# First weights of a seven-product group read from a copy at another SBUF place; ones kept as one column

## The chip, the cores and the metric

The kernel runs on one core of a Trainium2 chip. The metric is the device time of one execution in microseconds (us). A core has TensorE (PE, matrix products), VectorE (DVE), ScalarE (ACT), GpSimd (POOL) and SyncE (SP, which issues most transfers). A product on PE has two operands in SBUF: a stationary block of 128x128 weights, which is loaded first (PEld in the profile, overlapping the product before), and moving columns, which stream past it. Results go to PSUM.

## The reference, cut to what matters

The reference is a decoder trunk of two layers on 512 tokens with 1024 features, in float32. Each layer is: half a SwiGLU FFN, a mixer (gated linear attention, GLA, in the first layer; stick-breaking attention, SB, in the second), and half a SwiGLU FFN again, each behind an RMSNorm and added to x.

```python
def rmsnorm(x, g):
    y = x * lax.rsqrt(jnp.mean(x * x, axis=-1, keepdims=True) + EPS)
    return y * g

def swiglu(h, w_gate, w_up, w_down):
    return (jax.nn.silu(h @ w_gate) * (h @ w_up)) @ w_down

for i in range(2):
    x = x + 0.5 * swiglu(rmsnorm(x, ffn1_norm[i]), ffn1_w_gate[i], ffn1_w_up[i], ffn1_w_down[i])
    h = rmsnorm(x, mix_norm[i])
    x = x + (gla_mixer(h, ...) if i % 2 == 0 else sb_mixer(h, ...))
    x = x + 0.5 * swiglu(rmsnorm(x, ffn2_norm[i]), ffn2_w_gate[i], ffn2_w_up[i], ffn2_w_down[i])
return rmsnorm(x, final_norm)
```

w_gate and w_up are 1024x2816, w_down is 2816x1024. There are four FFNs in all.

## The kernel before, in words

x stays in SBUF transposed: eight tiles `x0` to `x7` of 128 features x 512 tokens. Every large product is made from three products of split operands: a tile is cut into a rounded part h (float32r) and the rest l, and W·B becomes Wh·Bh + Wl·Bh + Wh·Bl (`mm3`, whose products all carry line 62).

**The feed.** Weights pass through a queue of entries (`feed.q`), in the order in which the products are issued. An `Entry` has units, views of a chunk loaded by SP into `raw` (or `rawd` for the down projection). Before it is used, `Entry.split` cuts each unit: ACT casts it to `wh` (line 116), DVE subtracts to `wl` (line 118). `wh` and `wl` have four buffers each. `Feed.start` splits the entry at hand and up to two more behind it, at most four large units together, and begins to load chunks up to six entries ahead.

**Places.** A `wh` or `wl` buffer has 64 columns (256 bytes) to spare, and `place` says where in it the block begins: 0 for most entries, NEAR = 16 columns (64 bytes) for the entries of the seven-product form, NEAR_MOVING = 48 columns (192 bytes) for `tok` entries, where the weights' chunk is the moving operand. The tiles are laid out one behind the other, and all the large ones have sizes that are multiples of 256 bytes, or come behind such. So in this kernel an operand's place can be told by its address divided by 256: the remainder of a block at place 0 is that of the x, xh/xl, th/tl, nh/nl and hh/hl tiles, and is called remainder 0 here. Weights at NEAR have remainder 64, a `tok` chunk as moving operand has 192.

**An FFN.** The 2816 inner features are 11 chunks of 256, for gate and for up. The first three gate chunks and the first two up chunks go through `feat`: eight k-tiles of three products, 512 columns each (`ps_f`). All others go through `seven`: the product of a 2x2 block matrix of weights (256 features x 1024) with the 2x2 blocked input (1024 x 512 tokens) is computed with seven block products in place of eight (Winograd's form). Each block product is four k-tiles of three products with 256 columns, at line 500: 84 products a group, in PSUM tiles `ps_w`, `ps_z` and `ps_q`. A group has two entries:

- `body_1`: a11·n (ps_w), then sums s2 (ps_z), s1 (ps_q), then a12 (ps_w). Units: the chunk's first 128 columns and `sums_12`.
- `body_2`: s3 (ps_z), s4 (ps_q), a22 (ps_w). Units: `sums_34` and the last 128 columns of the chunk's second half.

DVE makes the sums of weight blocks (lines 485 to 492) and the sums of input blocks, which are split to `th`/`tl`. Between the groups stand entries of the down projection (`down`, product `ps_d`, 512 columns, 24 products an entry). So in the middle of an FFN PE does 84 products of 256 columns, 24 (or 48) of 512 columns, 84 of 256, and so on. There are 68 groups in the four FFNs; 52 follow a `ps_d` product, 4 a `ps_f` product and 12 another group directly.

**Ones.** `ones` is a 128x128 tile of 1.0, set by DVE at the start. It is the weights of `stats_b` (`ps_R`, spreads the norm factor over all partitions) and of the GLA output norm (`ps_on`), and its first column is the moving operand of `stats_a` (`ps_st`). `gT` (128x50) holds the norms' gains, copied from PSUM at the start; its first eight columns are used again by the last norm at the very end.

The SB layer's values and the GLA layer's use `tok` (`ps_t`): the input tile is the weights (remainder 0), the weights' chunk at NEAR_MOVING is the moving operand, 256 columns, three products a k-tile, 24 products a PSUM tile. In the GLA layer, `ps_gk` (the gate's first projection) has 512 columns with weights `gs`, a tile that by the sizes of those ahead of it has remainder 64.

Of the kernel before, what the change touches and what calls it, by code (L numbers as in the profile page):

```python
# [10 lines left out]
F32 = mybir.dt.float32  # L11
F32R = mybir.dt.float32r
# [6 lines left out]
P = 128  # L19
T = 512  # L20
D = 1024
KD = D // P
# [6 lines left out]
NEAR, NEAR_MOVING = 16, 48  # L29
# [3 lines left out]
def decoder(ctx: ExitStack, tc: tile.TileContext, a: dict, out: bass.AP):  # L33
    nc = tc.nc


    cp = ctx.enter_context(tc.tile_pool(name="cp", bufs=1))
    xp = ctx.enter_context(tc.tile_pool(name="xp", bufs=1))
    np_ = ctx.enter_context(tc.tile_pool(name="np", bufs=8))
    wp = ctx.enter_context(tc.tile_pool(name="wp", bufs=4))  # L40
# [6 lines left out]
    def psum(name, tag=None):  # L47
        if tag is None:
            tag = order[turn_[0] % 8]
            turn_[0] += 1  # L50
        return pp.tile([P, T], F32, tag=tag, bufs=banks[tag], name=name)
# [1 line left out]

    ident = cp.tile([P, P], F32, name="ident")
    make_identity(nc, ident)
    ones = cp.tile([P, P], F32, name="ones")
    nc.vector.memset(ones, 1.0)

    xs = [xp.tile([P, T], F32, name=f"x{k}") for k in range(KD)]

# [12 lines left out]
    class Chunk:  # L73
        def __init__(self, src, n, m):
            self.src, self.n, self.m, self.t = src, n, m, None
            self.pool = None
            self.few = False
# [12 lines left out]
    class Entry:  # L90
# [1 line left out]

        def __init__(self, units, body, place=0):
            self.units, self.body, self.W, self.place = units, body, None, place

        def split(self):
            if self.W is None:
                self.W = []  # L100
                for ch, view, n, m in self.units:
                    r = view(ch.load())
                    few = n * m < 1024
                    if few:

                        h = st["few"].tile([P, n * m + NEAR], F32R, tag="vh", bufs=1, name="wh")[:, NEAR:]
                        l = st["few"].tile([P, n * m + 64 - NEAR], F32R, tag="vl", bufs=1, name="wl")[:, : n * m]
                    else:
                        h, l = (
                            wp.tile([P, n * m + 64], F32R, tag="w" + t, bufs=4, name="w" + t)[  # L110
                                :, self.place : self.place + n * m
                            ]
                            for t in "hl"
                        )
                    h, l = (t.rearrange("p (n m) -> p n m", m=m) for t in (h, l))
                    st["cut"] = nc.scalar.copy(h, r).ins  # L116
                    with tc.issue_after(st["gains"]):
                        nc.vector.tensor_tensor(out=l, in0=r, in1=h.bitcast(F32), op=ALU.subtract)  # L118
                    self.W.append((h, l))

    class Feed:
        def __init__(self):
# [38 lines left out]
    feed = Feed()  # L161
# [162 lines left out]
    st = {}  # L324
# [89 lines left out]
    class FFN:  # L414
# [60 lines left out]
        def seven(self, ch, group=None):  # L475

            H = T // 2  # L480
            s12, v = [None], {}

            def sums_12(t):
                s = s12[0] = self.tp.tile([P, KD, P], F32, tag="s", bufs=4, name="s12")
                nc.vector.tensor_tensor(out=s[:, 0:4], in0=t[:, 0:4, P:], in1=t[:, 4:8, P:], op=ALU.add)
                nc.vector.tensor_tensor(out=s[:, 4:8], in0=s[:, 0:4], in1=t[:, 0:4, 0:P], op=ALU.subtract)
                return s

            def sums_34(t):
                s = self.tp.tile([P, KD, P], F32, tag="s", bufs=4, name="s34")  # L490
                nc.vector.tensor_tensor(out=s[:, 0:4], in0=t[:, 0:4, 0:P], in1=t[:, 0:4, P:], op=ALU.subtract)
                nc.vector.tensor_tensor(out=s[:, 4:8], in0=t[:, 4:8, 0:P], in1=s12[0][:, 4:8], op=ALU.subtract)
                return s

            def prod(o, w, w0, b, first=True):
                for j in range(4):
                    bh, bl = b(j)
                    wh, wl = w[0][:, w0 + j], w[1][:, w0 + j]
                    for n, (l_, r_) in enumerate(((wh, bh), (wl, bh), (wh, bl))):
                        nc.tensor.matmul(  # L500
                            o, l_, r_, start=first and j + n == 0, stop=j == 3 and n == 2, skip_group_check=True
                        )

            def half(k0, c):
                return lambda j: (st["h"][k0 + j][:, c * H : c * H + H], st["l"][k0 + j][:, c * H : c * H + H])

            def part(name):
                return self.tp.tile([P, H], F32, tag="c", bufs=2, name=name)

            def add(o, x, y):  # L510
                nc.vector.tensor_tensor(out=o, in0=x, in1=y, op=ALU.add)

            def left(o, w):
                if group is None:
                    nc.scalar.activation(o[:, 0:H], w, AF.Silu)
                else:
                    nc.vector.tensor_tensor(out=o[:, 0:H], in0=w, in1=self.gates[0][:, 0:H], op=ALU.mult)

            def rest(o, c):
                if group is None:  # L520
                    st["silu"] = nc.scalar.activation(o[:, c:T], o[:, c:T], AF.Silu).ins
                    self.gates.append(o)
                    return
                nc.vector.tensor_tensor(out=o[:, c:T], in0=o[:, c:T], in1=self.gates.pop(0)[:, c:T], op=ALU.mult)
                self.close(o, group)

            def body_1(W):
                ax, s = W

                v["w"], v["z"], v["q"] = psum("ps_w"), psum("ps_z"), psum("ps_q")  # L530
                w, z, q = (v[n][:, 0:H] for n in "wzq")
                v["o"] = self.tp.tile([P, T], F32, tag="t", name="o0")
                prod(w, ax, 0, half(0, 0))
                v["u2"] = part("u2")
                nc.scalar.copy(v["u2"], w)
                yield
                prod(z, s, 4, lambda j: self.t_half(1, j))
                add(v["u2"], z, v["u2"])
                yield
                prod(q, s, 0, lambda j: self.t_half(0, j))  # L540
                v["c5"] = part("c5")
                nc.scalar.copy(v["c5"], q)
                yield
                prod(w, ax, 4, half(4, 0), first=False)
                left(v["o"], w)
                yield

            def body_2(W):
                s, a22 = W
                q, y = v["q"][:, 0:H], v["z"][:, H:T]  # L550
                o0, o1 = v["o"], self.tp.tile([P, T], F32, tag="t", name="o1")
                prod(y, s, 0, lambda j: self.t_half(2, j))
                u3 = o1[:, 0:H]
                add(u3, y, v["u2"])
                nc.vector.tensor_tensor(out=o1[:, H:T], in0=u3, in1=v["c5"], op=ALU.add)
                yield
                prod(q, s, 4, half(4, 1), first=False)
                add(o0[:, H:T], q, v["u2"])
                rest(o0, H)
                yield  # L560
                o = v["w"][:, H:T]
                prod(o, a22, 0, lambda j: self.t_half(3, j))
                add(o1[:, 0:H], o, u3)
                rest(o1, 0)
                yield

            feed.q.append(Entry([(ch, lambda t: t[:, :, 0:P], KD, P), (ch, sums_12, KD, P)], body_1, NEAR))
            feed.q.append(Entry([(ch, sums_34, KD, P), (ch, lambda t: t[:, 4:8, P:], 4, P)], body_2, NEAR))

        def t_half(self, i, j):  # L570
# [575 lines left out]
                feed.entries(self.end + 2 - feed.pos)  # L1146

    gT = cp.tile([P, 50], F32, name="gT")  # L1150
    phases = []

    def ffn(n, i, gi, nxt, **kw):
# [49 lines left out]
    with tc.tile_pool(name="ip", bufs=1) as ip:  # L1203
# [10 lines left out]
        lead = phases[0].lead  # L1214
# [6 lines left out]
                c.load()  # L1221
        ps = psum("ps_g")
        nc.tensor.transpose(ps[:, 0:P], gl, ident)
        st["gains"] = nc.vector.tensor_copy(gT, ps[:, 0:50]).ins
        st["nh"], st["nl"], pst = [], [], []
        for hf in range(2):
            for k in range(hf * 4, hf * 4 + 4):
                ps = psum("ps_x")
# [73 lines left out]
```

## Time and profile before

| | us |
|---|---|
| median of 3 runs | 1896.93 (1896.65 to 1897.21) |
| the profiled execution | 1896.61 |
| its span | 1894.7 |
| PE busy | 1874.6 (99%) |
| weight loads busy (PEld) | 1672.7 (88%) |
| DVE busy | 1459.6 (77%) |
| ACT busy | 943.5 (50%) |
| mean granted TensorE clock | 0.998 |

The profiled execution is one run; 1.9 us of it lie outside the span. A line of a group reads: line of the kernel, engine, operation, out<-in by tile names, sizes and count, then the busy time in us, the mean ns of one, and the idle time of the engine just ahead of them. A line in order of time begins with the start and the duration in us. A matmul's duration contains its way through the array and overlaps the next one's, so how fast PE moves is read from start to start.

### The profile page before, as it was taken

The numbers are of one execution on the slowest core, as the hardware profiler recorded it, in microseconds if no ns is written. First come the engines' busy times: TensorE is split into PE (matmuls) and PEld (weight loads), VectorE is DVE, ScalarE is ACT, GpSimd is POOL, SyncE is SP. The second block draws the span as 40 slices with busy tenths as digits, with TensorE's granted clock in tenths as the row PEclk, the third lists the DMA queues.
The fourth block names the chain that finished last, engine by engine and source line by source line (L and its number), as shares of the span: only waits on it lengthen the run. The fifth ranks groups of instructions, "written<-read, shape, count | busy, mean of one in ns | idle before, by whom it ended". The sixth has DMA issues, their size and how long they took to land.

```text
span 1894.7 us, 28826 instructions
## 1 busy us (share of the span) xinstructions
PE 1874.6 (99%) x11789; PEld 1672.7 (88%) x11789; DVE 1459.6 (77%) x2313; ACT 943.5 (50%) x1450; POOL 7.4 (0%) x17
## 2 busy tenths in 40 slices
PE   8999999999999999999999999999999999999998
PEld 6899999889887899999989999998888788999997
DVE  7978777775766987877888778776878779777775
ACT  6534434444554544444453444445888755444444
POOL 0000000100000000000000000000000000000000
PEclk9999999999999999999999999999999999999999
DMA  5423333312223233332233333233221223333321
GB/s 156 145 91 110 101 112 96 91 46 67 67 67 111 89 90 113 106 116 79 78 112 122 101 100 108 82 90 100 67 67 58 66 90 104 107 101 103 119 80 67
DMA packets 177512, 179.02 MB, mean 94 GB/s; under 512 B 4034, under 2 KB 167924, under 8 KB 177380
## 3 DMA queue, kind: packets, MB, share of 16 engines
q1 hardware_dynamic: 176768, 176.18, 29.8%
q8 instruction: 92, 1.51, 0.3%
q0 software_dynamic: 512, 0.99, 0.2%
q14 instruction: 40, 0.33, 0.1%
q10 hardware_dynamic: 100, 0.03, 0.0%
HBM read 175.11 MB, written 2.10 MB: 94 GB/s over the span
## 4 chain that ended last, share of the span: by engine, by line
PE 96%; DVE 2%; ACT 1%; DMA 1%; issue 0%; DVEq 0%; ACTq 0%; SPq 0%
PE ps_d L62 24%; PE ps_f L62 20%; PE ps_w L500 15%; PE ps_q L500 10%; PE ps_z L500 10%; PE ps_t L62 5%; PE ps_b L62 4%; PE ps_S L62 1%; PE ps_z L1031 1%; PE ps_bt L62 1%; PE ps_oT L1093 1%; PE ps_T L1078 1%; PE ps_o L62 1%; DMA raw<-in_ffn_w_up_dram 0%; DVE wl L118 0%; DMA raw<-in_ffn_w_gate_dram 0%
## 5 line engine op out<-in xcount | busy, mean ns | idle before, releaser
L118 DVE TENSOR_TENSOR wl<-raw,wh 128x1024 fp32r<-128x1024 f32 x244 | 261.3, 1071 | 90.8 <-ACT wh L116 70.0
L116 ACT CAST wh<-raw 128x1024 fp32r<-128x1024 f32 x244 | 226.0, 931 | 139.9 <-PE ps_f L62 44.4
L62 PE MATMUL ps_d<-hh,wh 128*128 128x512 f32 x672 | 262.1, 390 | 0.0
L62 PE MATMUL ps_d<-hh,wl 128*128 128x512 f32 x672 | 262.1, 390 | 0.0
L62 PE MATMUL ps_d<-hl,wh 128*128 128x512 f32 x672 | 261.4, 389 | 0.0
L116 ACT CAST wh<-s 128x1024 fp32r<-128x1024 f32 x136 | 142.6, 1049 | 149.9 <-PE ps_q L500 81.9
L289 DVE SCALAR_TENSOR_TENSOR x<-ps_d,x 128x512 f32<-128x512 f32 x184 | 125.8, 688 | 96.2 <-PE ps_d L62 95.9
L118 DVE TENSOR_TENSOR wl<-s,wh 128x1024 fp32r<-128x1024 f32 x136 | 166.4, 1224 | 30.7 <-ACT wh L116 25.0
L62 PE MATMUL ps_f<-xh,wh 128*128 128x512 f32 x448 | 182.1, 407 | 2.8 <-DVE q L694 1.5
L62 PE MATMUL ps_f<-xl,wh 128*128 128x512 f32 x448 | 175.2, 392 | 0.0
L62 PE MATMUL ps_f<-xh,wl 128*128 128x512 f32 x448 | 174.7, 390 | 0.0
L116 ACT CAST wh<-rawd 128x1024 fp32r<-128x1024 f32 x84 | 88.3, 1051 | 157.0 <-PE ps_d L62 136.7
L500 PE MATMUL ps_w<-nh,wh 128*128 128x256 f32 x544 | 152.9, 281 | 0.0
L500 PE MATMUL ps_w<-nl,wh 128*128 128x256 f32 x544 | 152.9, 281 | 0.0
L500 PE MATMUL ps_z<-th,wh 128*128 128x256 f32 x544 | 152.9, 281 | 0.0
L500 PE MATMUL ps_z<-th,wl 128*128 128x256 f32 x544 | 152.9, 281 | 0.0
L500 PE MATMUL ps_z<-tl,wh 128*128 128x256 f32 x544 | 152.9, 281 | 0.0
L500 PE MATMUL ps_w<-nh,wl 128*128 128x256 f32 x544 | 152.8, 281 | 0.0
L62 PEld LDWEIGHTS ps_d<-hl,wh 128*128 128x128 f32 x672 | 126.2, 188 | 26.7
L62 PEld LDWEIGHTS ps_d<-hh,wh 128*128 128x128 f32 x672 | 126.1, 188 | 24.7
L62 PEld LDWEIGHTS ps_d<-hh,wl 128*128 128x128 f32 x672 | 126.4, 188 | 24.0
L118 DVE TENSOR_TENSOR wl<-rawd,wh 128x1024 fp32r<-128x1024 f32 x84 | 102.9, 1225 | 45.9 <-ACT wh L116 32.7
(246 smaller groups left out, 4697.5 us busy)
## 6 DMA issues: line engine op xcount, KB each, us to landing
raw<-in_ffn_w_gate_dram SPq DMA_DIRECT2D x43, 1024.0 KB, 5.4
raw<-in_ffn_w_up_dram SPq DMA_DIRECT2D x43, 1024.0 KB, 5.3
rawd<-in_ffn_w_down_dram SPq DMA_DIRECT2D x84, 512.0 KB, 3.5
raw<-in_gla_w_in_dram SPq DMA_DIRECT2D x12, 1024.0 KB, 5.4
raw<-in_sb_w_in_dram SPq DMA_DIRECT2D x16, 512.0 KB, 3.8
raw<-in_gla_w_out_dram SPq DMA_DIRECT2D x4, 1024.0 KB, 5.2
raw<-in_sb_w_in_dram SPq DMA_DIRECT2D x4, 1024.0 KB, 5.2
raw<-in_sb_w_out_dram SPq DMA_DIRECT2D x4, 1024.0 KB, 5.1
```

The costliest lines, as they stand in the source:

```text
L62: nc.tensor.matmul(ps, l, r, start=first, stop=last)
L116: st["cut"] = nc.scalar.copy(h, r).ins
L118: nc.vector.tensor_tensor(out=l, in0=r, in1=h.bitcast(F32), op=ALU.subtract)
L289: nc.vector.scalar_tensor_tensor(out=xs[k], in0=ps, scalar=0.5, in1=xs[k], op0=ALU.mult, op1=ALU.add)
L500: nc.tensor.matmul(o, l_, r_, start=first and j + n == 0, stop=j == 3 and n == 2, skip_group_check=True)
L1031: nc.tensor.matmul(o_, l_, r_, start=first, stop=last, skip_group_check=True)
L1078: nc.tensor.transpose(ps[:, c0 : c0 + P], ys[yb][:, yc + j * P : yc + (j + 1) * P], ident)
L1093: nc.tensor.matmul(po[e * 64 : e * 64 + 64, j * P : T], self.v[j][:, c : c + 64], self.wt[p, e][bk][:, c0 : c0 + n], start=j == 0, stop=j ...
```

## The change

There are two edits. First, an entry can be a `lead`. The first entry of a seven-product group is one when the entry ahead of it in the queue does not stand at NEAR, that is, when it isn't another group's. A lead entry's `split` makes one more tile, `w1` (128x128, one buffer, behind `raw` in its pool, at remainder 0): ACT casts the first k-tile's block of the first unit into it, behind the same unit's cast and subtraction. The first product of `body_1` (Wh of k-tile 0 with Bh) takes its weights from `w1`, with the same values as before; the other 83 products of the group are as they were.

Second, the 128x128 tile `ones` goes. `gT` is allocated first and gets a 51st column, set to 1.0, and `ones` is that column read by 128 columns. The 512 bytes a partition that this frees are those that `w1` takes.

```diff
@@ decoder
     make_identity(nc, ident)
-    ones = cp.tile([P, P], F32, name="ones")
-    nc.vector.memset(ones, 1.0)
+
+    gT = cp.tile([P, 51], F32, name="gT")
+    nc.vector.memset(gT[:, 50:51], 1.0)
+    ones = gT[:, 50:51].to_broadcast([P, P])
@@ Entry
-        def __init__(self, units, body, place=0):
+        def __init__(self, units, body, place=0, lead=False):
             self.units, self.body, self.W, self.place = units, body, None, place
+            self.lead = lead
@@ Entry.split
                     self.W.append((h, l))
+                    if self.lead and len(self.W) == 1:
+
+                        first = wp.tile([P, m], F32R, tag="w1", bufs=1, name="w1")
+                        nc.scalar.copy(first, r[:, 0])
+                        self.first = first
@@ FFN.seven
-            def prod(o, w, w0, b, first=True):
+            def prod(o, w, w0, b, first=True, lead=None):
                 for j in range(4):
                     bh, bl = b(j)
                     wh, wl = w[0][:, w0 + j], w[1][:, w0 + j]
                     for n, (l_, r_) in enumerate(((wh, bh), (wl, bh), (wh, bl))):
+                        if lead is not None and j + n == 0:
+                            l_ = lead
                         nc.tensor.matmul(
                             o, l_, r_, start=first and j + n == 0, stop=j == 3 and n == 2, skip_group_check=True
                         )
@@ body_1
-                prod(w, ax, 0, half(0, 0))
+                prod(w, ax, 0, half(0, 0), lead=entry.first if lead else None)
@@
-            feed.q.append(Entry([(ch, lambda t: t[:, :, 0:P], KD, P), (ch, sums_12, KD, P)], body_1, NEAR))
+
+            lead = feed.q[-1].place != NEAR
+            entry = Entry([(ch, lambda t: t[:, :, 0:P], KD, P), (ch, sums_12, KD, P)], body_1, NEAR, lead)
+            feed.q.append(entry)
@@
-    gT = cp.tile([P, 50], F32, name="gT")
@@
-        st["gains"] = nc.vector.tensor_copy(gT, ps[:, 0:50]).ins
+        st["gains"] = nc.vector.tensor_copy(gT[:, 0:50], ps[:, 0:50]).ins
```

## The prediction

> **What bounds the kernel now.** I read the page's busy line and chain first, then the costliest groups, then the order of time on PE in four stretches.
>
> ```profile
> PE 1874.6 (99%) x11789; PEld 1672.7 (88%) x11789; DVE 1459.6 (77%) x2313; ACT 943.5 (50%) x1450; POOL 7.4 (0%) x17
> ...
> PE 96%; DVE 2%; ACT 1%; DMA 1%; issue 0%; DVEq 0%; ACTq 0%; SPq 0%
> ...
> L62 PE MATMUL ps_d<-hh,wh 128*128 128x512 f32 x672 | 262.1, 390 | 0.0
> L500 PE MATMUL ps_w<-nh,wh 128*128 128x256 f32 x544 | 152.9, 281 | 0.0
> L500 PE MATMUL ps_z<-th,wl 128*128 128x256 f32 x544 | 152.9, 281 | 0.0
> ```
>
> PE is on the chain for 96% of the span and waits for nothing ahead of the seven-product groups (0.0 in the last column). So the kernel lasts as long as products follow each other, and the question is their distance from start to start; the mean of one (281 ns) overlaps its neighbours. There are 5712 products of 256 columns at line 500 (68 groups of 84). Their distance is 117.78 ns, taken from the starts of the 5656 that follow another of their kind.
>
> The next two fences are the order of time on PE, from the two halves of one column block of the SB layer's values (ps_t, also 256 columns):
>
> ```profile
> 1305.22 0.28 PE L62 MATMUL ps_t<-wh,xh 128*128 128x256 f32 x1
> ...
> 1310.17 0.28 PE L62 MATMUL ps_t<-wh,xh 128*128 128x256 f32 x1
> ```
> ```profile
> 1311.77 0.28 PE L62 MATMUL ps_t<-wh,xh 128*128 128x256 f32 x1
> ...
> 1316.53 0.28 PE L62 MATMUL ps_t<-wh,xh 128*128 128x256 f32 x1
> ```
>
> Each fence spans 42 products of the same tiles in the same order. The first takes 4.95 us, 117.9 ns each; the second 4.76 us, 113.3 ns each. **The same products have two steady rates.** Of the 29 stretches of ps_t, 26 settle at 113.3 and three at 117.8, each within its first six products, and none changes afterwards. How a stretch begins therefore decides its rate. All 68 seven-product groups run at the slow one. They are entered like this, and left like this:
>
> ```profile
> 106.72 0.39 PE L62 MATMUL ps_d<-hh,wl 128*128 128x512 f32 x1
> 106.95 0.39 PE L62 MATMUL ps_d<-hl,wh 128*128 128x512 f32 x1
> 107.18 0.28 PE L500 MATMUL ps_w<-nh,wh 128*128 128x256 f32 x1
> 107.30 0.28 PE L500 MATMUL ps_w<-nh,wl 128*128 128x256 f32 x1
> ...
> 117.07 0.40 PE L62 MATMUL ps_d<-hh,wh 128*128 128x512 f32 x1
> 117.30 0.40 PE L62 MATMUL ps_d<-hh,wl 128*128 128x512 f32 x1
> ...
> 118.46 0.39 PE L62 MATMUL ps_d<-hh,wh 128*128 128x512 f32 x1
> ```
>
> The 84 products from 107.18 to 117.07 take 117.7 ns each, from the first on: there is no settling. After the group, six 512-column products take 1.39 us where six at the settled 226.67 ns take 1.36; over all 56 exits this settling costs 27.6 ns each.
>
> **The beat.** 226.67, 113.33 and three times 117.78 (353.33) ns are 34, 17 and 53 times 6.667 ns. Divided by 6.667 ns, the starts of all settled 512-column stretches leave one common remainder, apart from a drift of 2.7 ns over the whole run. So products settle onto a common beat. A 512-column product settles exactly on it. The fast rate keeps one place on the beat, while the slow rate visits three places in turn.
>
> Now the entry. In the 56 groups that follow a 512-column product, the last distance before the group is 225.9 ns instead of 226.67. The only difference from an ordinary pair is that the weights loaded beside that last product stand 64 bytes off the place. So the group starts 0.8 ns ahead of the beat and goes straight into the slow cycle.
>
> **The change, part by part.**
>
> *The copied block.* The load beside the last 512-column product then has the same place as in any ps_d pair (remainder 0 instead of 64 in 256 bytes). Every settled ps_d pair measures 226.67, so the group's first product starts 0.7 to 0.8 ns later, on the beat: 56 x 0.75 = 0.04 us lost.
>
> Is on the beat where the fast rate lives? No settled stretch in the trace has the groups' own places, so I shift ps_t. There weights and moving columns both stand 64 bytes earlier than in the groups. In the slow cycle the remainders of ps_t's starts are on average 1.6 ns less than the groups' (3.9, 1.8, 0.0 against 5.8, 3.3, 1.5). The fast ps_t stretches start 1.6 ns before the beat. Shifted by the same 1.6, the groups' fast place is the beat itself, where the change puts the first product. Its weights are long loaded by then, and the next load starts about 3 ns after it, as in the fast stretches. Hence I take the fast rate from product one; the 12 groups that follow another group inherit it.
>
> Price: 5656 x (117.78 - 113.33) = **25.1 us**. The ends are nothing (the slow rate stays) and a loss (a rival below). I take the full value because ps_t is the nearest row: same width, and the same 64 bytes between weights and moving columns.
>
> *The exits.* The last product of a group is loaded over by ps_d weights at the other place, which I cannot see at the fast rate. Bounds: the 27.6 ns of settling stay, or they vanish because the group ends on the beat. A collision on that one product would cost a beat, 6.67 ns. I take "vanish, with one beat lost" (120.0 ns to the first ps_d product, now 117.4): 56 x (27.6 + 117.4 - 120.0) = 1.4 us gained; the ends are 0 and 1.8.
>
> *The copy on ACT*, 56 instructions of 128 columns. The 512- and 1024-column casts take 619 and 1050 ns, 0.84 per column, so 128 columns take about 296 ns: 16.6 us in all. The cover is ACT's idle half. The price without it would be those 16.6 us. Queued behind each copy is the cast of the next sums block. At 113.03 that cast would move to 113.33 and end by 114.4; its subtraction on DVE starts at 114.45 anyway, and PE wants the block at 122.5. PE's first product now waits for the copy as well, eight microseconds old by then. The buffer's previous reader is a group back, so the copy waits for nobody. Cost 0.
>
> *Ones as one column.* 48 products ps_R (6.4 us), 8 ps_on and 40 ps_st read it. No row shows a weight load that repeats one column. Bounds: ps_R's distance, 112 ns, falls to the 28 ns at which other short products are seen to start (-4.0 us), or doubles (+5.4). The nearest row is ps_S, which streams columns with a step and takes 267 ns against 275 with none, so 0. The smaller memset is start-up work. The gains copy follows it on DVE in program order anyway, and the column isn't written again.
>
> *Addresses.* x, xh/xl, wh/wl and raw move by 512 bytes, twice 256, so no place changes. wh's four buffers already differ by odd multiples of 256 with one rate. Cost 0. No DMA is added or moved on SP's or POOL's queue.
>
> *What is late next.* In an FFN (660 to 944 us) DVE is busy 221.7 of 284.0. With 6.6 us less it is at 80% and stays behind PE. The tight spot is the start of each FFN, where DVE is busy 40.95 of 41.00 us (30 to 71) but has caught up by 71.9. The worst case loses the gain of the first two groups, 4 x 168 x 4.44 ns = 3.0 us; I take 0.
>
> **Sum.** 25.1 + 1.4 - 0.04 = 26.5 us. The profiled execution took 1896.61, so 1870.1. The median of the runs stands 0.32 above it: **1870.4 us**, 1.4% less. About 0.2%, 3.8 us, is what a measurement can tell from no change.
>
> The Trainium skill, in "TensorE: Matmul & The Clock Gate", section "Step-by-step: what each phase is for", says that PE reads weights and moving operand through two independent ports, so loading the next weights takes nothing from the running matmul. By that rule a place of the weights could not matter, and the sum would be 1896.9, the first rival. The entry's 225.9 against 226.67 ns speaks against it. The same page's section "Back-to-back issue gap" gives N/2.4 + 2.5 ns, 109.2 for 256 columns. If the groups reached that estimate, the time would be about 1848; no stretch here is under 113.3.
>
> **The rivals.**
>
> *The groups stay slow.* The step from 0.8 ns ahead of the beat to the beat is small, and of the stretches of ps_t one went slow from a second product that I place about 0.4 ns past its fast point. Price 0: 1896.9. Against it: that product's predecessor was still waiting for its weights, which a 512-column product never does.
>
> *Partly fast.* Some groups lose the beat on an operand that comes late. At half the groups: 1896.9 - 13 = 1884. Against it: 0.0 waits in the groups, and ps_t never lost its rate.
>
> *A third, slower rate.* The gate's ps_gk products have 512 columns, weights 64 bytes off the moving place, and take 233.3 ns per product (370.9 to 374.6 us), one beat above 226.67. If the groups settle one beat above the fast rate, 120.0 ns, they cost 5656 x 2.22 = 12.6 us more: 1909.5. It decides from 118.5 ns on. Against it: no 256-column stretch settles there.
>
> **How the numbers follow.** Fast rate 0.76, partly 0.05, stays slow 0.12, third rate 0.07. The likeliest one's own range is 1866 to 1875: exits -0.4/+1.4, the FFN start +3, most of the ones column's -4/+5. The range reaches over the partly fast case to 1885, which holds 0.8. Faster 0.81, no difference 0.12, slower 0.07.
>
> **What would show it.** Right: line 500's rows fall from 281 to about 276 ns a matmul, a group from 9.89 to 9.53 us, the first product at 226.67 behind its predecessor, ps_d after a group at 227 at once, and 56 ACT rows of 128 columns near 0.3 us. Wrong: 281 still there (start-up does not decide, or the beat's place is misread), rows near 283 (third rate), PE waits on ACT at line 500 (the copy is late), or ps_R's row well above 6.4 us.

## The result, and the profile after

The changed kernel takes 1873.34 us (median, 1871.49 to 1873.78) where the kernel before, run beside it, takes 1897.07 (1896.65 to 1897.68). The ratio is 0.9873, with a 95% interval of 0.9856 to 0.989. Two later sets of runs gave 1871.56 beside 1896.96 (0.9868) and 1872.29 beside 1896.84 (0.9869). The forecast was 1870.4, in a range of 1866 to 1885.

The profiled execution is the lowest of the first set, 1871.49 us with a span of 1869.6. Its page, the busy line, the chain and three of the costliest groups:

```profile
PE 1849.7 (99%) x11789; PEld 1647.6 (88%) x11789; DVE 1456.8 (78%) x2313; ACT 954.0 (51%) x1506; POOL 7.3 (0%) x17
...
PE 96%; DVE 2%; ACT 1%; DMA 1%; issue 0%; DVEq 0%; ACTq 0%; SPq 0%
...
L64 PE MATMUL ps_d<-hh,wh 128*128 128x512 f32 x672 | 262.1, 390 | 0.0
...
L510 PE MATMUL ps_z<-th,wl 128*128 128x256 f32 x544 | 150.2, 276 | 0.0
...
L510 PE MATMUL ps_w<-nh,wl 128*128 128x256 f32 x544 | 150.1, 276 | 0.0
```

PE is as much on the chain as before and executes the same number of products. The groups' rows (line 500 before, 510 now) fell from 281 to 276 ns a product; ps_d's rows stand still. The whole gain is in the distance from one 256-column product to the next. The order of time on PE shows it at the group that was shown before (start and duration in us):

```profile
106.08 0.39 PE L64 MATMUL ps_d<-hh,wl 128*128 128x512 f32 x1
106.31 0.39 PE L64 MATMUL ps_d<-hl,wh 128*128 128x512 f32 x1
106.53 0.28 PE L510 MATMUL ps_w<-nh,w 128*128 128x256 f32 x1
106.65 0.28 PE L510 MATMUL ps_w<-nh,wl 128*128 128x256 f32 x1
...
116.05 0.40 PE L64 MATMUL ps_d<-hh,wh 128*128 128x512 f32 x1
116.29 0.40 PE L64 MATMUL ps_d<-hh,wl 128*128 128x512 f32 x1
...
117.44 0.39 PE L64 MATMUL ps_d<-hh,wh 128*128 128x512 f32 x1
```

From 106.53 to 116.05 the 84 products take 9.52 us, 113.3 ns each, where they took 9.89. The first product's weights are the copy (`w`). Behind the group, six ps_d products still take 1.39 us, as before. All distances below are taken from the starts in the traces, which are kept to the ns (the lines shown round them to 10 ns), as means over the groups.

| | before | after |
|---|---|---|
| last distance ahead of a group (56), ns | 225.95 | 226.66 |
| distance inside the groups (5656), ns | 117.78 | 113.36 |
| groups at the fast rate | 0 of 68 | 67 of 68, and one broken once |
| last product to first ps_d (56), ns | 117.38 | 113.36 |
| settling (what six ps_d products behind a group take over 6 x 226.67) (56), ns | 27.62 | 26.64 |

Inside the groups that is 5656 x 4.42 ns = 25.0 us, behind them 56 x (4.0 + 1.0) ns = 0.3, and the entry takes back 0.04. The sum, 25.3, stands beside a difference of spans of 25.1 (1894.7 and 1869.6). Against the medians of the same runs the gain is 23.7, 25.4 and 24.6 us in the three sets.

The two additions, as groups of instructions (busy us, mean ns, idle before), from the rows of ACT and of PE:

```profile
L126 ACT CAST w<-raw 128x128 fp32r<-128x128 f32 x56 | 16.4, 292 | 2.7 <-DMA raw<-in_ffn_w_up_dram 2.7
```
```profile
L64 PE MATMUL ps_R<-dg,gT 128*128 128x128 f32 x48 | 6.3, 274 | 0.0
```

The copies take 292 ns (296 forecast), and no wait of PE names one. The ones column costs ps_R nothing: 6.3 us here, 6.4 before.

### The profile page after: what moved, and what is told of

Read it like the earlier page. It is cut to its first block, busy times and chain, and to the rows that moved or that the text cites. A ratio compares the mean times of both kernels' runs of the same rounds, so it can differ in the third digit from the quotient of the medians.

```text
span 1869.6 us, 28889 instructions
## 1 busy us (share of the span) xinstructions
PE 1849.7 (99%) x11789; PEld 1647.6 (88%) x11789; DVE 1456.8 (78%) x2313; ACT 954.0 (51%) x1506; POOL 7.3 (0%) x17
## 4 chain that ended last, share of the span: by engine, by line
PE 96%; DVE 2%; ACT 1%; DMA 1%; issue 0%; DVEq 0%; ACTq 0%; SPq 0%
PE ps_d L64 25%; PE ps_f L64 20%; PE ps_w L510 15%; PE ps_z L510 10%; PE ps_q L510 10%; PE ps_t L64 5%; PE ps_b L64 4%; PE ps_S L64 1%; PE ps_z L1044 1%; PE ps_bt L64 1%; PE ps_oT L1106 1%; PE ps_T L1091 1%; PE ps_o L64 1%; DVE wl L121 0%; DMA raw<-in_ffn_w_up_dram 0%; PE ps_R L64 0%
## 5 line engine op out<-in xcount | busy, mean ns | idle before, releaser
L510 PE MATMUL ps_w<-nh,wh 128*128 128x256 f32 x488 | 134.7, 276 | 0.0
```

The source lines that it names most:

```text
L510: nc.tensor.matmul(o, l_, r_, start=first and j + n == 0, stop=j == 3 and n == 2, skip_group_check=True)
```

## The experiments

**The two edits apart.** One kernel has only the ones column; one has the whole change, with the copied block moved by 64 bytes, to where the other weights of the group begin.

```diff
 # ones only: the kernel before, and
+    ones = gT[:, 50:51].to_broadcast([P, P])
 # copy off its place: the changed kernel, and
-                        first = wp.tile([P, m], F32R, tag="w1", bufs=1, name="w1")
+                        first = wp.tile([P, m + NEAR], F32R, tag="w1", bufs=1, name="w1")[:, NEAR:]
-        v = sp.tile([P, n], F32, tag="rv", bufs=2, name="rv")
+        v = sp.tile([P, n], F32, tag="rv", bufs=1, name="rv")
-        y = sp.tile([P, n], F32, tag="ry", bufs=2, name="ry")
+        y = sp.tile([P, n], F32, tag="ry", bufs=1, name="ry")
```

> Only the second edit: ones as one column, no copied block. My theory (the place of the first block decides the group's rate): every group is entered 225.9 ns behind the last 512-column product and runs at 117.8 ns a product, the matmul rows of the groups stay at 281 ns, and the time is that of before, 1897 within 2 us. The rival that the column or the moved addresses bring the gain: rows at 276 ns and 1872 to 1874 us. If the repeated column made its loads dearer, ps_R's 48 products would be above 6.4 us and the time up to 5 us over before.

> The whole change, but the copied block stands 64 bytes further on, at the place of the group's other weights (the 64 bytes come out of two small buffers of the norms). Copies, waits and buffers are those of the change; the place alone is not. My theory: entry at 225.9 ns, all groups at 117.8 ns, rows at 281 ns, 1897 us. The rival that the separate buffer or the extra wait on ACT starts the group differently: 113.3 ns, rows at 276, 1873 us.

Ones only: 1896.93 (ratio 0.9999, 0.999 to 1.0009), all 68 groups at 117.8. Copy off its place: 1896.88 (0.9999, 0.9989 to 1.0008), last distance 225.96, all groups at 117.8. The page of the second has the group row of before:

```profile
L510 PE MATMUL ps_z<-th,wl 128*128 128x256 f32 x544 | 152.9, 281 | 0.0
```

The copy, its cast on ACT and PE's dependence on it are all there, and the gain is not. So the place of one block of 128 columns, 56 times, is worth the 25 us. The Trainium skill, in "TensorE: Matmul & The Clock Gate", section "Step-by-step: what each phase is for", has weights and moving columns read through independent ports; by it this kernel and the change should take the same time, and the trace doesn't agree.

**A copy for every group.** The 12 groups behind another group get one too: there its load runs beside a 256-column product, whose neighbours all have weights at 64.

```diff
-            lead = feed.q[-1].place != NEAR
+            lead = True
```

> All 68 groups read their first block from the copy, also the 12 that directly follow another group, where the load at the other place now runs beside a 256-column product. If the rate is set by the start alone and is stable against one off-place load, all stays at 113.3 ns and the time is that of the change (1873 us, at most 0.4 us more for settling). If one off-place load in the middle throws a stretch off the fast rate for good, these 12 groups run at 117.8 ns: 12 x 84 x 4.44 ns = 4.5 us more, 1877.8 us. I lean to the first, 0.6 to 0.4, since ps_t came back to the fast rate from most disturbances.

1877.31 (0.9896, 0.9876 to 0.9916): the 56 leading groups run at 113.3, the 12 others at 117.8, from the copy on. A pair of groups in the order of time:

```profile
71.76 0.28 PE L510 MATMUL ps_w<-nh,w 128*128 128x256 f32 x1
...
81.28 0.28 PE L510 MATMUL ps_w<-nh,w 128*128 128x256 f32 x1
...
91.17 0.39 PE L64 MATMUL ps_d<-hh,wh 128*128 128x512 f32 x1
```

The first 84 products take 9.52 us, the next 84 9.89. I had leaned to the opposite. One load at the wrong place puts a running stretch onto the slow rate, and in none of the 12 does it come back.

**The place of all the groups' weights.** The kernel before with NEAR at 0, 128 and 192 bytes in place of 64.

```diff
-NEAR, NEAR_MOVING = 16, 48
+NEAR, NEAR_MOVING = 0, 48      # then 32, 48 and 48, 48
```

> The kernel before with all weights of the groups at remainder 0, so that every load, not only the first, has the place of the moving columns. The entry is then on the beat, 226.67 ns. If the entry alone decides, the groups run at 113.3 ns and the time is 1872 us. If the 64 bytes between weights and moving columns are needed inside the group as well, the rate is above: one beat more, 120.0 ns, gives 5656 x 2.2 ns = 12.6 us over before, 1909 us. I expect the second.

> The kernel before with the groups' weights 128 bytes past the moving columns' place, in place of 64 (117.8 ns, 1896.9) or 0 (120.0 ns, 1909.3, the earlier run). If what counts is that the two differ: 117.8 ns again with an entry of 225.9 ns, 1896.9. If 128 keeps the 512-column product of the entry on the beat and the groups out of each other's way: 113.3 ns from the first product, 1872. If 128 counts as 0 for the reads (a period of 128 bytes): 120.0 ns, 1909.3. I have no row for it; 0.4, 0.3, 0.3.

> The kernel before with all weights of the groups 192 bytes past the moving columns' place (64: 117.8 ns and 1896.9; 0 and 128: 120.0 ns and 1909 to 1911). If odd multiples of 64 keep the two reads apart and the even ones don't: 117.8 or 113.3 ns by the entry, 1896.9 or 1872, the second without any copy. If only 64 does: 120.0 ns, 1909 to 1911. 0.35 for 117.8, 0.3 for 113.3, 0.35 for 120.

At 0: 1909.33 (1.0065, 1.0045 to 1.0085). At 128: 1911.42 (1.0076, 1.0056 to 1.0097). At 192: 1895.55 (0.9994, 0.9984 to 1.0005). The group rows at 0 and at 128, from their pages:

```profile
L500 PE MATMUL ps_z<-th,wl 128*128 128x256 f32 x544 | 154.0, 283 | 0.0
```
```profile
L500 PE MATMUL ps_z<-th,wl 128*128 128x256 f32 x544 | 154.5, 284 | 0.0
```

Inside the groups the distance settles at 120.0 ns at both, at 0 for every product and at 128 as the mean of 117.5, 120.0 and 122.5 in turn: the third rate of the rivals exists, and it is what the groups get when the weights stand 0 or 128 bytes from the moving columns. At 0 the first product does start on the beat (0.1 ns behind it), and its group runs at 120.0 all the same: the entry alone is not enough, the weights inside the group need their 64 bytes as well. At 192 they run at 117.8, as at 64, with a last distance of 225.84; behind the group the settling is 10.0 ns there in place of 27.6, which is the 1.0 us of the difference that can be read.

**The place of the copy.** The changed kernel with the copied block at 128 and at 192. The buffers of four small tiles of the norms are made single for the first (not shown below), and the copy lies in a stats tile for the second, so that the operands of the large products keep their places.

```diff
-                        first = wp.tile([P, m], F32R, tag="w1", bufs=1, name="w1")
+                        first = wp.tile([P, m + 32], F32R, tag="w1", bufs=1, name="w1")[:, 32:]
 # and, in the other kernel
+                        first = sp.tile([P, m + 48], F32R, tag="ss", name="w1")[:, 48:]
```

> The change with the copied block 128 bytes past the place of the ps_d weights, where the change has it at 0 and the earlier run had it at 64. If only the moving operand's own place (0) lets the last 512-column product end on the beat: first distance 225.9 ns, all groups at 117.8, 1896.9. If it is 64 alone that disturbs it: 226.67 ns, 113.3, 1873.3. If at 128 it is a beat late (233.3, as the gate's products): the group begins on the beat all the same, 113.3, 1873.7. I lean to the second, 0.5, against 0.35 for the first.

> The change with the copied block 192 bytes past the place of the ps_d weights (0 in the change: first distance 226.67 ns, 113.3 ns a product; 64: 225.9 and 117.8; 128: 232.5, then 113.3 after three products). Theory A (the phase of the first start against the beat decides alone) has already a hole: at 64 and at 128 the group starts at the same 5.8 ns of the 6.67, and one goes slow, the other fast. Theory B (64 is the one place that leads to the slow rate): first distance 226.7 or 233, 113.3 ns, 1871 to 1874. Theory C (odd multiples of 64 alike): 225.9, 117.8, 1896.9. I lean to B, 0.6.

At 128: 1874.13 (0.988, 0.986 to 0.99). At 192: 1897.20 (1.0001, 0.9991 to 1.0012), last distance 225.84, all groups at 117.8: as at 64, against my lean. The entry at 128, in the order of time:

```profile
106.77 0.40 PE L64 MATMUL ps_d<-hl,wh 128*128 128x512 f32 x1
107.00 0.28 PE L510 MATMUL ps_w<-nh,w 128*128 128x256 f32 x1
107.12 0.28 PE L510 MATMUL ps_w<-nh,wl 128*128 128x256 f32 x1
107.25 0.28 PE L510 MATMUL ps_w<-nl,wh 128*128 128x256 f32 x1
107.36 0.28 PE L510 MATMUL ps_w<-nh,wh 128*128 128x256 f32 x1
107.48 0.28 PE L510 MATMUL ps_w<-nh,wl 128*128 128x256 f32 x1
```

The last ps_d product takes 232.5 ns, and the group then needs 122.5, 121.7 and 115.9 ns for its first three products before it runs at 113.3. (Two of its groups lose the fast rate later on, at a late operand; see below.) Here is the hole in my reason. Counted from the settled ps_d starts, the first product starts 5.9 ns into the 6.67 ns beat with the copy at 64, 5.9 at 192 and 5.8 at 128: the same place. Two go slow and one goes fast. So the start of the first product does not decide alone.

**The exit.** The mirror of the change: the first ps_d product behind a group takes its weights from a copy at the groups' place, 64 bytes on, beside the change itself run again.

```diff
@@ Entry.split
+                    if self.after:
+                        first = sp.tile([P, P + NEAR], F32R, tag="ss", name="w2")[:, NEAR:]
+                        nc.scalar.copy(first, r[:, 0, 0:P])
+                        self.first = first
@@ down
+                    if after and m + f == 0:
+                        mm(ps, entry.first, hs[f][0], True, False)
+                        mm(ps, wl[:, f, s], hs[f][0], False, False)
+                        mm(ps, wh[:, f, s], hs[f][1], False, f == nf - 1)
+                        continue
@@
+        after = feed.q[-1].place == NEAR
+        entry = Entry([(ch, lambda t: t, nf, nd * P)], body, after=after)
```

> The change, and the mirror of it at the exit: the first product of the ps_d entry behind a group takes its weights from a copy that ACT makes at the groups' place (64 bytes on). Theory A (the settling behind a group comes from the ps_d weights that are loaded at the other place beside the group's last 256-column product): the load is now in place, the 26.6 ns of settling go at each of the 56 exits, 1.5 us, so 1871.8 where the change has 1873.3. The ps_d load behind it then runs beside a 512-column product and costs nothing. Theory B (the settling belongs to the change of width, 256 to 512 columns): it stays 26.6 ns and the time stays 1873.3. Theory C: the weights at 64 beside the first 512-column product move the next start off the beat, as at the entry before the change, and the settling only changes place: 20 to 35 ns, 1873.3. The timing can hardly tell 1.5 us; the distances in the profile can.

> The change once more, beside the next kernel, because the first profile of it came out 1.9 us under the median of its runs. Either theory: median 1872 to 1874, all leading groups at 113.3 ns a product, the first distance of a group 226.67 ns, 26.6 ns of settling at an exit. If the profile sits under the median by something in the kernel (a late operand in some executions), this profile may land near 1873.5 and then shows in which stretch the 2 us lie; if it is the execution as a whole, all stretches are longer by 0.1%.

1870.00 (1869.50 to 1871.35) with the exit's copy, 1871.56 (1871.20 to 1873.22) for the change beside it; ratios to before 0.986 (0.9843 to 0.9876) and 0.9868 (0.9853 to 0.9883). The intervals overlap, as forecast; the distances don't leave a doubt. The exit in the order of time, with the copied block `w`:

```profile
115.91 0.39 PE L64 MATMUL ps_d<-hh,w 128*128 128x512 f32 x1
116.13 0.39 PE L64 MATMUL ps_d<-hh,wl 128*128 128x512 f32 x1
...
117.27 0.39 PE L64 MATMUL ps_d<-hh,wh 128*128 128x512 f32 x1
```

Six products take 1.36 us in place of 1.39. Over the 56 exits the settling is 0.0 ns in place of 26.6, 1.5 us, and the spans differ by 1.3 (1868.0 and 1869.3). So the settling comes from the ps_d weights at 0 that are loaded beside the last 256-column product, and not from the change of width. This version has the lowest time of all.

**Copy and groups at 192.** The last kernel joins the copy at 0 with the place 192 for the groups.

```diff
-NEAR, NEAR_MOVING = 16, 48
+NEAR, NEAR_MOVING = 48, 48
```

> The change with the groups' other weights 192 bytes past the moving columns' place in place of 64; the copied block stays at 0. Odd multiples of 64 have behaved alike inside the group and at the entry, and at 192 the exit cost 10.0 ns in place of 27.6. If they are alike here too: first distance 226.67, 113.3 ns a product, and the exit at 10 ns in place of 26.6, 0.9 us under the change (1871.5 where that has 1872.4). If the fast rate needs 64: 117.8 or 120.0 ns, 1896 or 1909. If the exit's 10.0 ns belonged to the slow cycle's last phase, the time of the change. 0.5 for the first, 0.2 and 0.3 for the others.

1872.71 (0.9871, 0.9855 to 0.9888): last distance 226.62, 67 groups at 113.3, settling 26.8. At 192 the fast rate is there as at 64, and the 10.0 ns were not: they went with the slow cycle, my third case.

**The two microseconds between executions.** The twelve runs of the change lie between 1870.97 and 1873.78.

> The change a third time, for the 2 us between its executions (1871.2 to 1873.8 in eight). If this profile lands above 1872.5 it shows whether the time lies in waits on PE at the FFNs' starts (the ACT wait of ps_f was 1.6 in place of 0.4 us in the kernel of 1874.4) and in groups that lose an operand (0.2 us each), or in all stretches alike; under 1872 it adds nothing and the scatter stays open.

This profile landed at 1872.65 (span 1870.9), the one before it at 1871.26 (1869.3). The waits of PE (us in total, times, longest), of the longer one and of the shorter one:

```profile
PE ps_f L64 <- ACT wh L119: 1.6, 1, 1.6
...
PE ps_z L510 <- DVE u L521: 0.2, 1, 0.2
```
```profile
PE ps_f L64 <- ACT wh L119: 0.4, 1, 0.4
```

The wait for a cast at the first FFN's start is 1.2 us longer, but it doesn't add to the time: the transposes of x ahead of it (ps_x) take 1.2 us less, and behind both the longer execution is 0.6 us late, which is what its first transfer was late (6.4 and 5.8 us). Two groups that wait for an operand make another 0.5 of the 1.6, and 0.5 I can't place; it lies in steps of at most 0.2 us. It is no rate: all other groups are at 113.3 in both. That the runs without a profile differ in the same way was not seen. The line of ps_z is new, and the order of time on DVE and on PE shows where it is from:

```profile
1077.64 0.69 DVE L493 TENSOR_TENSOR s<-raw 128x512 f32<-128x512 f32 x1 [1.52 <-DMA raw<-in_ffn_w_gate_dram]
1078.25 0.68 DVE L499 TENSOR_TENSOR s<-raw 128x512 f32<-128x512 f32 x1
1078.85 0.42 DVE L521 TENSOR_TENSOR u<-ps_z,u 128x256 f32<-128x256 f32 x1
```
```profile
1078.88 0.28 PE L510 MATMUL ps_w<-nl,wh 128*128 128x256 f32 x1
1079.32 0.39 PE L510 MATMUL ps_z<-th,wh 128*128 128x256 f32 x1 [0.16 <-DVE u L521]
```

DVE takes the sums of weight blocks in program order. The first of two waits 1.5 us for a gate chunk from memory; behind them stands the read of ps_z, and behind that `body_2`, whose first product needs the PSUM tile: 435 ns from start to start. That group goes back to 113.3. In the kernel with copy and 192 the same place of the same FFN took 690 ns from start to start, and the products behind it ran on at 117.8 to the end of the group, 0.85 us in all. It was not alone: with the copy at 128, two groups had such a gap, of 407 and of 195 ns, and ran on at 117.8 too. Over all profiles of kernels with the copy at 0 or 128, seven groups were interrupted. Four came back to 113.3 (the late product 149, 156, 209 and 435 ns behind its predecessor), all in the change or with the exit's copy added; these three did not. So the length of the gap alone doesn't decide; what does, these runs don't show.

## Why the prediction was right

- *The main term.* 5656 x (117.78 - 113.33) = 25.1 us was forecast, 25.0 measured. What carried it was that the same products have two steady rates in one trace, and that the way in decides: the experiment with the copy 64 bytes off shows the second part on the groups themselves.
- *The reason given for it* was half right. The place of the load beside the last 512-column product is the cause. The step from there, that the rate follows from where the first product starts on the beat, is refuted: 5.8 to 5.9 ns into the beat led to the slow rate twice and to the fast rate once. What tells the copy at 128 from 64 and 192, the records don't show. It stays open. The place of the fast rate itself was worked out rightly by the shift from ps_t: in the change the settled starts of the groups lie on the beat to within 0.1 ns, and with the copy at 128 they do so once the first products are past.
- *The entry*: 226.66 where 226.67 was forecast.
- *The exits* are the mis-sized term: "vanish, with one beat lost", 1.4 us, measured 0.3. The settling stayed (26.6 of 27.6 ns) and the beat was not lost (113.36, not 120.0). I took the settling for a matter of where the group ends; it comes from the load of ps_d weights at 0 beside a 256-column product, which the change left as it was. The bounds, 0 and 1.8, held it.
- *Copy, ones column, addresses*: 0, as taken. For the ones column this was a guess that came true: the row of ps_S that it leaned on (267 ns) has 64 moving columns, the 275 beside it 128, so the two don't tell what a step costs; ps_R's own row, 6.3 us for 6.4, does. *DVE at the FFN's start*: no wait at the groups' line in the first two groups, but later ones wait in some executions, 0.07 to 0.85 us a group; I looked at the wrong place, the size was inside the 3.0.
- *The rivals.* "Stay slow" is what the copy does at 64 and at 192. "A third, slower rate" is what the groups do at 0 and at 128, 1909 to 1911, where 1909.5 had been worked out. "Partly fast" happened to three groups in two kernels, with the copy at 128 and with copy and groups at 192, each behind a late operand. None is what the change does.
- *The remaining distance.* The profiled executions of the change (1871.5, 1871.3, 1872.7) are 1.2 to 2.6 us over the 1870.1 worked out for one. In each 1.1 us of this is the exit term; the third has the later first transfer and the two interrupted groups besides. Against the medians the forecast is 1.2 to 2.9 us low.

The estimate of 109.2 ns by the Trainium skill's "TensorE: Matmul & The Clock Gate", section "Back-to-back issue gap", was reached in none of these runs: no settled stretch of 256 columns is under 113.3.

## What to carry to other kernels

Where PE is the bound and never waits, compare the distance from start to start of products of one shape across stretches: two steady rates in one trace are a reserve, and the shorter one is what the chip does with the same work. Then look at the SBUF place (address in 256 bytes) of the weights that are loaded beside each product, at the first and the last of a stretch above all, since one load in 84 set the rate of all that followed. Once a stretch is faster, look again for what stands in one queue behind a transfer.

## What the runs showed of the hardware

Places are those of the weights against the moving columns of the product beside which they are loaded.

| weights loaded at | 0 | 64 | 128 | 192 |
|---|---|---|---|---|
| beside the last 512-column product: its distance, ns | 226.66 | 225.96 | 232.5 | 225.84 |
| and the group behind it, weights at 64, ns | 113.3 | 117.8 | 113.3, after three products | 117.8 |
| all loads beside 256-column products: distance, ns | 120.0 | 117.8, or 113.3 with the copy | 120.0 | 117.8, or 113.3 with the copy |

So the 256-column products go fastest with the next weights 64 or 192 bytes away, and only if the stretch is entered rightly. For 512 columns, settled ps_d products with all weights at 0 take 226.67 ns and the gate's ps_gk, with weights at 64, 233.3 (before); a single load at 64 or 192 doesn't lengthen its own product but leads the group behind it to the slow rate. At the seam of the two widths one copied block at the entry and one at the exit give each neighbour the place at which it settles best. The three rates of 256 columns are 17, 17 2/3 and 18 times 6.67 ns. Why the two widths differ in this was not tried; nor were places other than multiples of 64 bytes.
